# Two more blocks of each norm's modulation as dot products, and head and softmax scaling moved to ScalarE, in a hybrid DiT step

## The chip, the cores and the metric

One Trainium2 chip, one core. The metric is the device time of one launch in microseconds (us), the median of several runs. The engines are TensorE (PE, with its weight loads as PEld), VectorE (DVE), ScalarE (ACT), GpSimd (POOL) and SyncE (SP, which here only issues DMAs).

## The reference

One layer of a diffusion backbone, on 128 context tokens (stream s=0) and 128 latent tokens (s=1), width 2048, in fp32. The six modulation vectors of a stream come from its condition; RMSNorm is scaled and shifted with them before each sub-layer:

```python
sh1, sc1, g1, sh2, sc2, g2 = ada_mod(c, w_ada, b_ada)      # silu(c) @ w_ada + b_ada, split in 6
h = rms_norm(x, norm1_w) * (1 + sc1) + sh1
qa, ka, va, qb, kb, vb, ga, gb = project_heads(h, w_in, ...) # q and k are RMS-normed per head of 128
...                                                          # softmax attention, mixers A and B
x = x + g1 * merge_branches(oa, ob, ga, gb, w_br_a, w_br_b, w_out)
h2 = rms_norm(x, norm2_w) * (1 + sc2) + sh2
x = x + g2 * (relu(h2 @ w_up) ** 2 @ w_down)
```

Mixer A is windowed attention with two key heads and a sink logit in the softmax, mixer B a neighbourhood attention with eight heads and a position bias; latent queries also see a cache of 128 context keys.

## The kernel before, in words

**Steps.** All large products run over a list of *steps*, 456 in all: one weight tile of 128 x 1024 fp32 (512 KB), 12 matmuls of 512 columns each. For precision each weight is used as a high part and a low part: ACT copies the tile into wH (`copy`, line 101), DVE subtracts to wL (line 260), and three matmuls (wH·hH, wL·hH, wH·hL) replace one. For steps in the table `LO_DMA` the low part is made without DVE: ACT writes the negative of wH (line 266) and a POOL DMA loads the weight once more and adds it (line 267).

**Order of the steps.** `begin` does steps 0 to 2; then the input projection runs in chunks of its 16 k-tiles (`CHUNKS`, 2, 2, 2, 4, 6), so that it can start before all of the modulated input h exists: steps 0 to 8 need k-tiles 0 and 1, 9 to 17 the next two, then 18 to 26, 27 to 44 and 45 to 71. The gates are steps 72 to 135, the branch products 136 to 167, the output product 168 to 199, the rest the two layers of the MLP.

**Modulation.** Shift and scale of a block of 128 columns (an *fb*) come in one of two ways. *As matmuls*: `mod_pair` loads eight tiles of w_ada ("araw") for two blocks (`pair_load`, line 322), multiplies them with the padded conditions (`pair_mm_q`, line 330: the profile counts 64 per pair), copies the result to SBUF (`ada_evac`), transposes it back into columns (`ada_cols`, line 348, into "ps_sel") and finishes with three small DVE operations (lines 351 to 358). `make_h` then modulates xnT (ACT line 378, DVE line 376) and `split_h` makes hL (line 105). The first `FB1` blocks of norm 1 go this way, pair f at step `ADA_AT[f]` (pair 0 in `begin`), and the first `FB_DVE` blocks of norm 2, half a pair at each step of `SS_AT`. *As dot products*: `dot_load` (line 1398) loads transposed rows of w_ada ("aT"), `load_cond` (line 1392) spreads half a condition over the partitions ("cB", two tiles), and DVE reduces the product to one column per stream (`dot`, line 1411). The rest of the blocks go this way, and so do the gates g1 and g2. A dot job takes two dots at neighbouring steps; each block needs two jobs for shift and two for scale.

**Attention.** `qk_stat` squares q or k (ACT, line 671), reduces per head (DVE, line 673) and takes the inverse root; `qk_apply` scales the heads of stream 0 on ACT (line 683) and those of stream 1 on DVE (line 684). There are seven such units, 26 heads per stream. An attention job has the stages scores (PE, line 756), softmax (ACT exponentials with accumulated sums, line 781), `normalise` (DVE scales four rows of probabilities at once, line 795), transposed probabilities (PE line 802, copied by ACT into "probT") and values (PE, line 809 for mixer A, 813 for B); eight jobs, four rows of 128 or 256 each.

**What sets the order.** Each engine executes in program order. At step i, `run` first issues the loads of all steps up to i + RUN[i] on SP's queue, then prepares high and low parts up to i + LOOK[i], then issues the matmuls, then whatever the tables put at that step: `DOTS1` (dots of norm 1), `DOTS` (of g1 and norm 2), `DOTS2` (of g2), `ADA_AT`, `SS_AT`, `POST` (stat, apply and transpose of each unit), `JOBS` (the five stages of the eight jobs). SP's queue is in that order too, and a few transfers are in flight at once.

Of the kernel before, what the change touches and what calls it, by code (L numbers as in the profile page):

```python
# [47 lines left out]
GATE2_USE = 3  # L48
ROW_AT = [5, 5, 9, 5]
DIRECT = (3,)  # L50
LO_DMA = [88, 106, 116, 131, 165, 180, 184, 196, 218, 224, 230, 232, 250, 251, 256, 282, 283, 288, 314, 315, 320, 329, 346, 347, 352, 378, 379, 384, 392, 410, 416, 442, 443, 449, 450]
LO_AHEAD = 2

LOOK = "652322414122454322223333333122333442223323122555465644344534355765215632223444456685566655544323333333321122122312343545666445443333342344444444444434556566643344457766322234414766567565566546555331235663226676666666656665554444444444444444555555555555555544433333333344445555555555555555444444444444444455555555555555554444433244444444555555555555555546444444444444445555555555555555444444444445555555666465555555554444446656654585434443744464222433444444"
RUN = "411111111111121323334444433333333312222233465566655466545667777556664445555776765655445445555656776654432333333312444444555566553333333343334455555566655655555655666575565577788866677666665653476544343366555566666666666666665555555555554444566666666666666655555555555555556666666666666666555555555555555566666666555666665555577555555555666666666666666655555555555555556666666666666666555577755555575454566666676555566666666665555555776766555535444666666666"
CONST_AT = [65, 69]
ADA_AT = [None, 5, 13, 16, 21, 37, 32]
XS_AT = {1: 13, 2: 19, 3: 31}
POST = {('kvA', 0): [67, 71, 76], ('qA', 0): [70, 73, 78], ('qA', 1): [72, 74, 83], ('kB', 0): [76, 86, 90], ('qB', 0): [82, 84, 93], ('kB', 1): [87, 90, 98], ('qB', 1): [90, 93, 96]}
JOBS = [[80, 81, 81, 88, 94], [79, 83, 88, 90, 92], [87, 87, 89, 95, 100], [93, 93, 96, 102, 105], [96, 97, 100, 105, 112], [102, 103, 107, 112, 123], [105, 107, 111, 118, 123], [112, 115, 118, 121, 123]]  # L60
SS_AT = [44, 57, 75, 75, 139, 139]
T_AT = [3, 4]
PREP_IN = [5, 7]
DOTS = [32, 44, 47, 47, 49, 50, 51, 52, 53, 56, 58, 60, 67, 67, 68, 69, 77, 78, 84, 85, 92, 93, 93, 94, 95, 99, 100, 103, 103, 104, 108, 110, 111, 111, 116, 118, 120, 120, 121, 122, 126, 126, 128, 129, 130, 132, 134, 137, 137, 138, 138, 143, 144, 145, 151, 155, 155, 158, 160, 160, 166, 167, 173, 173, 174, 175, 176, 178, 179, 180, 183, 190]
DOTS2 = [234, 237, 240, 266, 269, 272, 298, 301, 329, 330, 332, 363, 364, 367, 397, 398, 424, 426, 426, 428, 429, 431, 431, 432, 432, 436, 439, 439, 440, 441, 444, 444]
STAT_AT = [-1, 0, 8, 11]
T_PAIR = [[6, 8], [6, 8], [8, 10], [5, 7], [10, 13], [8, 14], [12, 9]]
# [10 lines left out]
def tile_hybrid_step(ctx: ExitStack, tc: tile.TileContext, a):  # L78
# [98 lines left out]
    r = SM(2, "r")  # L177
# [104 lines left out]

    by_dma = sorted(LO_DMA)

    def run():
        loads.sort(key=lambda x: x[:2])
        for st in wsteps:
            while loads and loads[0][0] <= st["i"] + int(RUN[st["i"]]):
                loads.pop(0)[2]()
            for j in sorted(j for j in pre if j <= st["i"]):  # L290
                for fn in pre.pop(j):
                    fn()
            to = st["i"] + int(LOOK[st["i"]]) + 1
            while by_dma and by_dma[0] < to + LO_AHEAD:
# [372 lines left out]
    def qk_stat(u, nh):  # L667
        raw = units[u]
        sq = G("sq").rearrange("p (s h d) -> p s h d", s=2, d=HD)[:, :, 0:nh, :]
        for s in range(2):  # L670
            act.activation(sq[:, s].rearrange("p h d -> p (h d)"), raw[:, s, 0:nh * HD], AF.Square)
        ssq, r = SM(2 * nh, "ssq"), SM(2 * nh, "rq")
        dve.tensor_reduce(ssq.rearrange("p (s h) -> p s h", s=2), sq, axis=AX.X, op=OP.add)
        rsqrt(r, ssq, HD * EPS)
        qk[u] = sq, r

    def qk_apply(u, nh):

        name, raw = u[0], units[u]
        x4 = raw.rearrange("p s (h d) -> p s h d", d=HD)[:, :, 0:nh, :]  # L680
        sq, r = qk.pop(u)
        for h in range(nh):
            act.activation(x4[:, 0, h, :], x4[:, 0, h, :], AF.Copy, scale=r[:, h:h + 1])
        dve.tensor_tensor(x4[:, 1], x4[:, 1], r[:, nh:2 * nh].unsqueeze(2).to_broadcast([P, nh, HD]), op=OP.mult)
# [47 lines left out]
    def att_job(mix, s, g):  # L732
        st = {}
        nb = 1 + s
        nk = P * nb
# [53 lines left out]
        def normalise():  # L789
            den, prob = st["den"], st["P"]  # L790
            if mix == "A":
                dve.tensor_tensor(den, den, st["es"], op=OP.add)
            rd = SM(4, "rd")
            dve.reciprocal(rd, den)
            dve.tensor_tensor(prob[:, :, 0:nk], prob[:, :, 0:nk], rd.unsqueeze(2).to_broadcast([P, 4, nk]), op=OP.mult)
# [706 lines left out]
    ex(placed[-1][0] + 2, dot_end)  # L1502
# [104 lines left out]
```

## Time and profile before

| | |
|---|---|
| median of 3 runs | 1323.73 us (1323.15 to 1325.13) |
| profiled execution | 1324.28 us |
| its span | 1322.5 us |
| busy in the span: PE, DVE, ACT, POOL | 1309.0, 1151.4, 890.8, 87.1 us |
| DMA traffic | 419.03 MB, 317 GB/s on the mean, 408 GB/s between 33 and 132 us |
| matmul records of the modulation pairs (line 330) | 640, 38.5 us busy |

The span is what the profiler sees between the first and the last instruction; the execution's time is 1.78 us longer. A busy time is the sum of an engine's instructions with overlaps removed. In the groups, "idle before" is how long the engine had stood still when the group's instructions began, and the arrow names what ended it. In the timelines consecutive instructions of one kind are one row, with their count behind an x. "SPq" and "POOLq" are the queues on which DMAs are issued.

### The profile page before, as it was taken

What the parts mean: (1) busy time and instruction counts of PE and PEld (TensorE: products, weight loads), DVE (VectorE), ACT (ScalarE), POOL (GpSimd) and SP (SyncE); (2) the same over time, 40 slices, a digit from 0 to 9 for tenths busy, and PEclk for the clock granted to TensorE, in tenths of its full rate; (3) what the DMA queues carried; (4) which work ended last, traced back from release to release, by engine and by line L of the source; (5) the groups of instructions that cost most, each with busy time, mean ns of one, the idle gap of its engine ahead of it and who ended that gap; (6) DMA issues with size and microseconds to landing.
All of it is one profiled execution on the core that took longest, in us unless ns stands there. A gap on an engine that the chain in (4) does not pass through costs nothing.

```text
span 1322.5 us, 18220 instructions
## 1 busy us (share of the span) xinstructions
PE 1309.0 (99%) x6388; PEld 1061.3 (80%) x6388; DVE 1151.4 (87%) x1487; ACT 890.8 (67%) x1129; POOL 87.1 (7%) x109
## 2 busy tenths in 40 slices
PE   8999999999999999999999999999999999999998
PEld 4777788788888878888888888888888888888876
DVE  4578699988898999999789889898898998979996
ACT  5634656576565545755788877968879688796772
POOL 0000000512000000000100010100101001010011
PEclk9999999999999999999999999999999999999999
DMA  9999998887689999998489998888998799899996
GB/s 375 408 408 409 406 398 344 326 286 281 200 296 343 373 377 349 323 374 306 137 289 291 290 312 273 283 300 289 292 321 281 282 341 288 295 269 366 375 334 185
DMA packets 155260, 419.03 MB, mean 317 GB/s; under 512 B 52720, under 2 KB 53984, under 8 KB 155168
## 3 DMA queue, kind: packets, MB, share of 16 engines
q1 hardware_dynamic: 146128, 386.54, 80.1%
q0 software_dynamic: 8848, 31.23, 10.3%
q8 instruction: 50, 0.82, 0.2%
q14 instruction: 42, 0.34, 0.1%
q10 hardware_dynamic: 192, 0.10, 0.0%
HBM read 390.24 MB, written 17.61 MB: 308 GB/s over the span
## 4 chain that ended last, share of the span: by engine, by line
PE 93%; DMA 3%; DVE 2%; issue 1%; POOL 0%; ACT 0%; POOLq 0%; DVEq 0%; ACTq 0%
PE acc L313 16%; PE acc L314 16%; PE acc L315 16%; PE Q L1191 6%; PE Q L1192 6%; PE Q L1193 6%; PE acc L424 5%; PE acc L425 5%; PE acc L426 5%; PE ps_ada L330 2%; DMA araw<-in_w_pair 2%; PE ps_S L756 1%; DMA wL<-in_w_down 1%; DVE aT L1411 1%; PE acc L1026 1%
## 5 line engine op out<-in xcount | busy, mean ns | idle before, releaser
L101 ACT ACTIVATE wH<-raw 128x1024 fp32r<-128x1024 f32 (+1 forms) x376 | 381.0, 1045 | 126.4 <-DMA raw<-in_w_in 17.0
L260 DVE TENSOR_TENSOR wL<-raw,wH 128x1024 fp32r<-128x1024 f32 x335 | 399.1, 1223 | 47.8 <-ACT wH L101 32.7
L424 PE MATMUL acc<-wH,hH 128*128 128x512 f32 x276 | 109.1, 395 | 0.0
L426 PE MATMUL acc<-wH,hL 128*128 128x512 f32 x276 | 107.6, 390 | 0.0
L425 PE MATMUL acc<-wL,hH 128*128 128x512 f32 x276 | 107.5, 390 | 0.0
L313 PE MATMUL acc<-wH,hH 128*128 128x512 f32 x256 | 102.6, 401 | 0.0
L315 PE MATMUL acc<-wH,hL 128*128 128x512 f32 x256 | 99.8, 390 | 0.0
L314 PE MATMUL acc<-wL,hH 128*128 128x512 f32 x256 | 99.7, 390 | 0.0
L1411 DVE CUSTOM_DVE_ANT_0 junk<-aT,cB,cols 128x1024 bf16<-128x1024 f32 x56 | 71.3, 1283 | 1.4 <-DMA cB<-silu 1.4
L1411 DVE CUSTOM_DVE_ANT_0 aT<-aT,cB,cols 128x1024 f32<-128x1024 f32 x56 | 71.6, 1288 | 0.2
L424 PEld LDWEIGHTS acc<-wH,hH 128*128 128x128 f32 x276 | 51.8, 188 | 13.6 <-issue 3.3
L1256 DVE TENSOR_TENSOR tL<-t,tH 128x1024 fp32r<-128x1024 f32 x42 | 51.2, 1220 | 11.2 <-ACT tH L101 11.2
L426 PEld LDWEIGHTS acc<-wH,hL 128*128 128x128 f32 x276 | 51.8, 188 | 11.2 <-DVE hL L105 0.2
L101 ACT ACTIVATE uH<-raw 128x1024 fp32r<-128x1024 f32 x42 | 44.4, 1058 | 23.6 <-DVE raw L1250 21.5
L425 PEld LDWEIGHTS acc<-wL,hH 128*128 128x128 f32 x276 | 51.9, 188 | 10.3
L101 ACT ACTIVATE tH<-t 128x1024 fp32r<-128x1024 f32 x42 | 44.3, 1054 | 23.5 <-DVE t L1246 18.5
L313 PEld LDWEIGHTS acc<-wH,hH 128*128 128x128 f32 x256 | 48.1, 188 | 10.5 <-issue 1.1
L314 PEld LDWEIGHTS acc<-wL,hH 128*128 128x128 f32 x256 | 48.1, 188 | 10.0 <-issue 0.7
L315 PEld LDWEIGHTS acc<-wH,hL 128*128 128x128 f32 x256 | 48.1, 188 | 10.1
L1246 DVE TENSOR_TENSOR t<-raw 128x1024 f32<-128x1024 f32 x42 | 51.2, 1218 | 1.0 <-PE acc L314 1.0
L1238 DVE TENSOR_TENSOR XL<-raw,XH 128x1024 fp32r<-128x1024 f32 x42 | 51.2, 1218 | 0.6 <-DMA sm<-dsum 0.5
L1256 DVE TENSOR_TENSOR uL<-raw,uH 128x1024 fp32r<-128x1024 f32 x42 | 51.1, 1218 | 0.0
(630 smaller groups left out, 3374.4 us busy)
## 6 DMA issues: line engine op xcount, KB each, us to landing
raw<-in_w_in SPq DMA_DIRECT2D x133, 512.0 KB, 9.0
raw<-in_w_down SPq DMA_DIRECT2D x128, 512.0 KB, 6.6
raw<-in_w_upF SPq DMA_DIRECT2D x84, 512.0 KB, 6.3
araw<-in_w_pair SPq DMA_DIRECT2D x80, 512.0 KB, 10.1
aT<-in_w_gT SPq DMA_DIRECT2D x64, 512.0 KB, 8.9
aT<-in_w_adaT SPq DMA_DIRECT2D x48, 512.0 KB, 9.9
raw<-in_w_up SPq DMA_DIRECT2D x44, 512.0 KB, 6.2
raw<-in_w_out SPq DMA_DIRECT2D x32, 512.0 KB, 10.2
```

The costliest lines, as they stand in the source:

```text
L101: act.activation(out, in_, AF.Copy)
L260: dve.tensor_tensor(st["lo"], st["raw"], st["hi"].bitcast(F32), op=OP.subtract)
L313: pe.matmul(acc[tb], sh, wh[:, k, :], start=f, stop=False, **kw)
L314: pe.matmul(acc[tb], sh, wl[:, k, :], start=False, stop=False, **kw)
L315: pe.matmul(acc[tb], sl, wh[:, k, :], start=False, stop=l, **kw)
L424: pe.matmul(acc[tb], sh, wh[:, k, :], start=kt == 0 and k == 0 and not held and not seeded, stop=False, **kw)
L425: pe.matmul(acc[tb], sh, wl[:, k, :], start=False, stop=False, **kw)
L426: pe.matmul(acc[tb], sl, wh[:, k, :], start=False, stop=last and k == 1 and not hold, **kw)
L1191: pe.matmul(acc, stat[0], hi, start=f, stop=False)
L1192: pe.matmul(acc, stat[0], lo, start=False, stop=False)
L1256: dve.tensor_tensor(b[n + "L"], v, b[n + "H"].bitcast(F32), op=OP.subtract)
L1411: dve.tensor_tensor_reduce(out, box["raw"], cB[s, tag], 1.0, dst if second else baT[:, part, fb:fb + 1], OP.mult, OP.add, dst)
```

## The change

- `FB1` 14 to 12 and `FB_DVE` 6 to 4: two blocks of norm 1 (one pair) and two of norm 2 (two half pairs) become dot products. 16 araw loads and 64 matmuls less in the program (128 of the profile's records, which count each twice), 16 more aT loads, 32 more dots.
- `qk_stat`: a square per head with an accumulated sum on ACT (52) in place of 14 squares and seven DVE reductions. `qk_apply`: ACT scales the heads of both streams, DVE no longer does. `normalise`: four ACT copies with a scale per job in place of one DVE operation.
- Tables anew. Pair 1 stands at step 3, no longer at 5; the dots of norm 1 are 16 jobs from step 8 on, formerly 8 from step 26 on; five more steps have their low part by DMA; `LOOK` and `RUN` differ in many places.

```diff
-FB_DVE = 6
-FB1 = 14
+FB_DVE = 4
+FB1 = 12
-DOTS1 = [26, 26, 29, 36, 39, 40, 41, 42]
+DOTS1 = [8, 8, 9, 12, 16, 18, 23, 26, 27, 28, 31, 31, 33, 35, 37, 39]
-LO_DMA = [88, 106, 116, 131, 165, 180, 184, 196, 218, 224, 230, 232, ..., 384, 392, 410, 416, 442, 443, 449, 450]
+LO_DMA = [46, 57, 74, 92, 106, 114, 116, 127, 165, 176, 184, 196, ..., 385, 410, 411, 416, 440, 442, 449]
-ADA_AT = [None, 5, 13, 16, 21, 37, 32]
+ADA_AT = [None, 3, 13, 16, 21, 35]
-SS_AT = [44, 57, 75, 75, 139, 139]
+SS_AT = [75, 75, 139, 139]
...
+        ssq, r = SM(2 * nh, "ssq"), SM(2 * nh, "rq")
         for s in range(2):
-            act.activation(sq[:, s].rearrange("p h d -> p (h d)"), raw[:, s, 0:nh * HD], AF.Square)
-        ssq, r = SM(2 * nh, "ssq"), SM(2 * nh, "rq")
-        dve.tensor_reduce(ssq.rearrange("p (s h) -> p s h", s=2), sq, axis=AX.X, op=OP.add)
+            for h in range(nh):
+                act.activation(sq[:, s, h, :], raw[:, s, h * HD:(h + 1) * HD], AF.Square,
+                               accum_out=ssq[:, s * nh + h:s * nh + h + 1])
...
-        for h in range(nh):
-            act.activation(x4[:, 0, h, :], x4[:, 0, h, :], AF.Copy, scale=r[:, h:h + 1])
-        dve.tensor_tensor(x4[:, 1], x4[:, 1], r[:, nh:2 * nh].unsqueeze(2).to_broadcast([P, nh, HD]), op=OP.mult)
+        for s in range(2):
+            for h in range(nh):
+                act.activation(x4[:, s, h, :], x4[:, s, h, :], AF.Copy, scale=r[:, s * nh + h:s * nh + h + 1])
...
-            dve.tensor_tensor(prob[:, :, 0:nk], prob[:, :, 0:nk], rd.unsqueeze(2).to_broadcast([P, 4, nk]), op=OP.mult)
+            for h in range(4):
+                act.activation(prob[:, h, 0:nk], prob[:, h, 0:nk], AF.Copy, scale=rd[:, h:h + 1])
```

Lines of the changed kernel stand two further down behind the tables' place for `dot` and its helpers (1394, 1400, 1413), one or two further in attention. Two places where the order moves:

SP's queue near the start of the program, before: the loads (issuing line, destination<-source, shape, how many) behind the first pair's, with pair 1 (the first araw row), pair 2 and pair 3.

```order
L230 DMA raw<-in_w_in 128x1024 x6
L322 DMA araw<-in_w_pair 128x1024 x8
L230 DMA raw<-in_w_in 128x1024 x8
L322 DMA araw<-in_w_pair 128x1024 x8
L230 DMA raw<-in_w_in 128x1024 x3
L322 DMA araw<-in_w_pair 128x1024 x8
```

The same place in the changed kernel, from pair 1 to pair 2:

```order
L230 DMA raw<-in_w_in 128x1024 x4
L322 DMA araw<-in_w_pair 128x1024 x8
L230 DMA raw<-in_w_in 128x1024
L1394 DMA cB_384<-silu 128x1024
L1394 DMA cB_386<-silu 128x1024
L230 DMA raw<-in_w_in 128x1024 x3
L1400 DMA aT<-in_w_adaT 128x1024 x2
L230 DMA raw<-in_w_in 128x1024
L1400 DMA aT<-in_w_adaT 128x1024
L230 DMA raw<-in_w_in 128x1024 x3
L1400 DMA aT<-in_w_adaT 128x1024
L230 DMA raw<-in_w_in 128x1024 x2
```

And from there, pair 2 to pair 3:

```order
L322 DMA araw<-in_w_pair 128x1024 x8
L230 DMA raw<-in_w_in 128x1024 x2
L1400 DMA aT<-in_w_adaT 128x1024
L230 DMA raw<-in_w_in 128x1024
L322 DMA araw<-in_w_pair 128x1024 x8
```

Pair 1 stands two step tiles further ahead; two condition broadcasts and four aT tiles have come in ahead of pair 2, one more aT tile ahead of pair 3.

ACT's queue in attention, before, from the squares of one unit of k to the copies of the second job's probabilities (the last row):

```order
L671 ACTIVATE sq<-u_kB_2335 128x512 x2
L781 ACTIVATE prob,den<-ps_S,nm 128x128 x4
L787 ACTIVATE es<-es 128x4
L101 ACTIVATE probT<-ps_PT 128x512
L101 ACTIVATE wH<-raw 128x1024 x2
L101 ACTIVATE T_kB_3124<-ps_qT 128x512
L715 ACTIVATE T_kB_3124<-ps_qT,cols 128x512
L683 ACTIVATE u_kB_2335<-u_kB_2335,rq 128x128 x4
L671 ACTIVATE sq<-u_qB_2179 128x512 x2
L101 ACTIVATE probT<-ps_PT 128x512 x2
```

The same stretch of the changed kernel:

```order
L673 ACTIVATE sq,ssq<-u_kB_2263 128x128 x8
L782 ACTIVATE prob,den<-ps_S,nm 128x128 x4
L788 ACTIVATE es<-es 128x4
L101 ACTIVATE probT<-ps_PT 128x512
L797 ACTIVATE prob<-prob,rd 128x256 x4
L797 ACTIVATE prob<-prob,rd 128x128 x4
L101 ACTIVATE wH<-raw 128x1024 x2
L101 ACTIVATE T_kB_3116<-ps_qT 128x512
L716 ACTIVATE T_kB_3116<-ps_qT,cols 128x512
L673 ACTIVATE sq,ssq<-u_qB_2102 128x128 x8
L101 ACTIVATE probT<-ps_PT 128x512 x2
```

Two rows of eight squares stand where two of two stood, and the softmax scalings of two jobs (L797) have come in between; the scaling of the k unit's heads (L683) has moved behind the copies.

More of the change, by code (lines that the diff above doesn't have):

```diff
@@ L50 @@
 DIRECT = (3,)
-LO_DMA = [88, 106, 116, 131, 165, 180, 184, 196, 218, 224, 230, 232, 250, 251, 256, 282, 283, 288, 314, 315, 320, 329, 346, 347, 352, 378, 379, 384, 392, 410, 416, 442, 443, 449, 450]
+LO_DMA = [46, 57, 74, 92, 106, 114, 116, 127, 165, 176, 184, 196, 218, 224, 228, 232, 237, 250, 251, 256, 282, 283, 288, 314, 315, 320, 329, 346, 347, 352, 378, 379, 384, 385, 410, 411, 416, 440, 442, 449]
 LO_AHEAD = 2
-LOOK = "652322414122454322223333333122333442223323122555465644344534355765215632223444456685566655544323333333321122122312343545666445443333342344444444444434556566643344457766322234414766567565566546555331235663226676666666656665554444444444444444555555555555555544433333333344445555555555555555444444444444444455555555555555554444433244444444555555555555555546444444444444445555555555555555444444444445555555666465555555554444446656654585434443744464222433444444"
@@ L55 @@
[L55 removed]
+LOOK = "652322403022443232223333212232333432223344255866576742122334355654104521223444356685566655544323344444432222122312343544555334333333342344444433444434556566643344457544102234414766567565676546555331235663226676666666656665543233333344444444555555555566666655533333333344445555555555555555444444444444443454444455555555554444433244444444555555555555555546444444444444447555555555555555444444444445555555666465555555554444346656654565434444754464233555555555"
@@ L56 @@
+RUN = "411111111111121323334466733333333312222344576677656467645667777556553434435865876875445445555656876654432333333312444444555566575533333343334455555566655655555655666575565577788866677666665653476544343366555566666666665555565555555555554466566666666666666655555555555555556666666666666666555555555555555566666666777777776555577555555555666666666666666655555555555555556666666666666666555555556666655474566666676555566666666665755555776777555534444666666666"
 CONST_AT = [65, 69]
-ADA_AT = [None, 5, 13, 16, 21, 37, 32]
+ADA_AT = [None, 3, 13, 16, 21, 35]
@@ L58 @@
 XS_AT = {1: 13, 2: 19, 3: 31}
-POST = {('kvA', 0): [67, 71, 76], ('qA', 0): [70, 73, 78], ('qA', 1): [72, 74, 83], ('kB', 0): [76, 86, 90], ('qB', 0): [82, 84, 93], ('kB', 1): [87, 90, 98], ('qB', 1): [90, 93, 96]}
-JOBS = [[80, 81, 81, 88, 94], [79, 83, 88, 90, 92], [87, 87, 89, 95, 100], [93, 93, 96, 102, 105], [96, 97, 100, 105, 112], [102, 103, 107, 112, 123], [105, 107, 111, 118, 123], [112, 115, 118, 121, 123]]
-SS_AT = [44, 57, 75, 75, 139, 139]
+POST = {('kvA', 0): [67, 71, 76], ('qA', 0): [70, 73, 78], ('qA', 1): [72, 74, 83], ('kB', 0): [76, 86, 90], ('qB', 0): [80, 84, 93], ('kB', 1): [87, 91, 99], ('qB', 1): [90, 93, 96]}
@@ L62 @@
+JOBS = [[80, 81, 81, 88, 94], [79, 83, 88, 90, 92], [87, 87, 88, 95, 100], [92, 93, 96, 102, 105], [96, 97, 100, 105, 112], [102, 103, 107, 112, 123], [105, 107, 111, 118, 123], [112, 115, 118, 121, 123]]
+SS_AT = [75, 75, 139, 139]
 T_AT = [3, 4]
 PREP_IN = [5, 7]
-DOTS = [32, 44, 47, 47, 49, 50, 51, 52, 53, 56, 58, 60, 67, 67, 68, 69, 77, 78, 84, 85, 92, 93, 93, 94, 95, 99, 100, 103, 103, 104, 108, 110, 111, 111, 116, 118, 120, 120, 121, 122, 126, 126, 128, 129, 130, 132, 134, 137, 137, 138, 138, 143, 144, 145, 151, 155, 155, 158, 160, 160, 166, 167, 173, 173, 174, 175, 176, 178, 179, 180, 183, 190]
@@ L65 @@
-DOTS2 = [234, 237, 240, 266, 269, 272, 298, 301, 329, 330, 332, 363, 364, 367, 397, 398, 424, 426, 426, 428, 429, 431, 431, 432, 432, 436, 439, 439, 440, 441, 444, 444]
+DOTS = [41, 44, 47, 47, 48, 48, 50, 51, 56, 56, 57, 58, 60, 62, 67, 67, 69, 69, 70, 73, 77, 79, 84, 84, 86, 92, 93, 93, 94, 95, 98, 99, 100, 103, 103, 106, 108, 111, 111, 112, 114, 116, 116, 118, 120, 120, 121, 122, 126, 126, 128, 129, 130, 132, 134, 137, 137, 138, 138, 143, 144, 144, 151, 155, 155, 158, 160, 160, 166, 167, 173, 173, 174, 175, 176, 178, 179, 183, 188, 190]
@@ L66 @@
+DOTS2 = [234, 237, 240, 266, 269, 272, 297, 301, 329, 330, 332, 363, 364, 367, 397, 398, 424, 426, 426, 428, 431, 431, 432, 432, 433, 436, 439, 439, 440, 441, 444, 444]
 STAT_AT = [-1, 0, 8, 11]
-T_PAIR = [[6, 8], [6, 8], [8, 10], [5, 7], [10, 13], [8, 14], [12, 9]]
-P_PAIR = [[1, 3], [2, 4], [3, 4], [-1, 3], [3, 4], [3, 6], [6, 4]]
+T_PAIR = [[10, 8], [6, 8], [8, 10], [5, 7], [10, 13], [8, 14], [12, 9]]
+P_PAIR = [[1, 3], [2, 4], [3, 4], [-1, 3], [3, 4], [3, 6], [6, 5]]
 M_TE = (3,)
@@ L72 @@
 P_UP = [2, 3]
-T_UP = [6, 11]
+T_UP = [7, 12]
 COL = {"qA": 0, "kvA": 1024, "qB": 1536, "kB": 2560, "vB": 3584, "gA": 4608, "gB": 6656}
```

## Prediction

> **What bounds the kernel now.** I read the page first: the busy line and the chain.
>
> ```profile
> span 1322.5 us, 18220 instructions
> PE 1309.0 (99%) x6388; PEld 1061.3 (80%) x6388; DVE 1151.4 (87%) x1487; ACT 890.8 (67%) x1129; POOL 87.1 (7%) x109
> PE 93%; DMA 3%; DVE 2%; issue 1%; POOL 0%; ACT 0%; POOLq 0%; DVEq 0%; ACTq 0%
> ```
>
> TensorE (PE) is the bound: 99% busy, 93% of the chain, some 13.5 us of the span without a matmul. So a matmul that goes is worth its own time, unless PE then waits for something that used to be just in time. Windows (start and end, length, then busy time of PE, PEld, DVE, ACT and POOL, clock, DMA share, GB/s) show where that is likely.
>
> ```profile
> 0.00:33.00 33.00, 28.84 (x178) 14.23 (x179) 15.76 (x34) 17.29 (x32) 3.11 (x12) 1.00 0.96 375
> 33.00:66.00 33.00, 32.37 (x193) 24.50 (x195) 16.89 (x23) 20.11 (x29) 0.00 (x0) 1.00 1.03 408
> ...
> 165.00:198.00 33.00, 33.00 (x170) 26.48 (x169) 32.86 (x46) 18.65 (x25) 0.00 (x0) 1.00 1.01 398
> ```
>
> ```profile
> 264.00:429.00 165.00, 165.00 (x848) 138.09 (x841) 143.85 (x208) 104.04 (x199) 15.21 (x13) 1.00 0.80 281
> 66.00:165.00 99.00, 99.00 (x684) 75.90 (x677) 74.64 (x116) 50.08 (x72) 0.00 (x0) 1.00 1.03 408
> ```
>
> To 198 us the DMA engines are as full as PE (share 1.01 to 1.03). VectorE (DVE) has 24 us free in 66 to 165, none in 165 to 198. In the attention stretch, 264 to 429, ScalarE (ACT) is idle for 61 us of 165, and PE for none. The longest waits of PE itself are few (total, times, longest):
>
> ```profile
> PE acc L314 <- DMA wL<-in_w_down: 1.7, 1, 1.7
> PE ps_ada L330 <- DMA araw<-in_w_pair: 1.3, 2, 0.7
> ```
>
> **The change, part by part.** *Matmuls removed.* The chain of waits has the modulation matmuls as pieces (start, us, what); PE's timeline has the selections, which make columns of them.
>
> ```profile
> 32.38 10.16 DMA araw<-in_w_pair
> 65.85 3.59 PE ps_ada L330 x64
> 171.70 1.86 PE ps_ada L330 x32
> 209.15 1.86 PE ps_ada L330 x32
> ```
>
> ```profile
> 30.27 0.39 PE L424 MATMUL acc<-wH,hH 128*128 128x512 f32 x1
> ...
> 38.53 3.42 PE L330 MATMUL ps_ada<-araw,early 128*32 128x256 f32 x56
> 42.58 0.64 PE L330 MATMUL ps_ada<-araw,early 128*32 128x256 f32 x8 [0.63 <-DMA araw<-in_w_pair]
> 43.15 0.50 PE L424 MATMUL acc<-wH,hH 128*128 128x512 f32 x1
> ...
> 46.03 0.60 PE L348 MATMUL ps_sel<-ident,S 128*128 128x128 f32 x4
> 46.38 0.48 PE L424 MATMUL acc<-wH,hH 128*128 128x512 f32 x1
> ...
> 78.25 3.66 PE L330 MATMUL ps_ada<-araw,early 128*32 128x256 f32 x64
> ```
>
> One pair of norm 1 goes (3.59), two half pairs of norm 2 (1.86 each, at steps 44 and 57) and two selections of four (46.03 to 46.38, 0.35 each, and about 0.1 of slower first matmuls behind it): 3.59 + 3.72 + 0.9 = **−8.2 us**, all on PE.
>
> *Loads of the first pairs.* Here I take more than half of it back. While the DMA engines are full, a tile lands when its place in SP's queue says. Pair 1's last tile is the chain's piece at 32.38: issued then, landed at 42.5, and PE's last eight matmuls start at 42.58, having waited for it. At 408 GB/s a 512 KB tile takes 1.285 us. The change puts those loads behind four step tiles instead of six, so the last lands 2 × 1.285 earlier, at 40.0, and its matmuls end at 40.6. But it puts the matmuls behind step 3 instead of step 5. Step 3 starts at 30.27 and is 12 matmuls 0.227 apart, 2.73 us, so PE is ready for pair 1 at 33.0 and stands waiting for tiles. Steps 4 and 5 (5.5 us), which used to cover this, come after it: step 6 starts at 46.1 instead of 43.15. **+2.9 us.**
>
> Pair 3 is next; SP's timeline (start, us, what) has the loads of pairs 2 and 3:
>
> ```profile
> 43.89 9.29 SPq L322 DMA_DIRECT2D araw<-in_w_pair  x8
> 54.12 2.87 SPq L230 DMA_DIRECT2D raw<-in_w_in  x3
> 57.94 9.24 SPq L322 DMA_DIRECT2D araw<-in_w_pair  x8
> ```
>
> Its last tile is issued at 67.1 and lands near 77.2, one microsecond before PE takes the pair at 78.25. In SP's new order, 36 tiles stand from pair 1's last to pair 3's last, where 27 did: two broadcasts of the condition (cB) and five aT tiles for the early dot products have come in. So it lands at 40.0 + 36 × 1.285 = 86.2 and its matmuls end at 86.8; PE, ready at 78.25 + 2.9, would have ended at 84.8. **+1.9 us.** Pair 2 stays covered: its last tile lands at 40.0 + 24 × 1.285 = 70.8, and PE, at it from 68.8, needs it only at 72. The pair after these is shifted no further by the queue than PE is. What is lost so early stays lost, for PE has no idle time to make it up in. Sum **+4.8**; bounds 0 (the queue moves faster than I count) and +8 (DVE late as well, next).
>
> *DVE.* By line and shape (busy us, mean ns, idle before):
>
> ```profile
> L260 DVE TENSOR_TENSOR wL<-raw,wH 128x1024 fp32r<-128x1024 f32 x335 | 399.1, 1223 | 47.8 <-ACT wH L101 32.7 <-PE acc L314 8.0 <-PE acc L315 3.7
> L1411 DVE CUSTOM_DVE_ANT_0 aT<-aT,cB,cols 128x1024 f32<-128x1024 f32 x56 | 71.6, 1288 | 0.2
> L673 DVE TENSOR_REDUCE ssq<-sq 128x8 f32<-128x1024 f32 (+1 forms) x7 | 8.0, 1139 | 2.2 <-ACT sq L671 2.2
> L684 DVE TENSOR_TENSOR u_kB<-u_kB,rq 128x512 f32<-128x512 f32 x2 | 1.4, 686 | 0.0
> L795 DVE TENSOR_TENSOR prob<-prob,rd 128x1024 f32<-128x1024 f32 x4 | 4.9, 1224 | 0.1
> L795 DVE TENSOR_TENSOR prob<-prob,rd 128x512 f32<-128x512 f32 x4 | 2.8, 692 | 0.1
> ```
>
> Thirty-two dot products come in (41 us). The seven reductions (8.0), seven scalings of 0.69 or less (4.5), the eight softmax scalings (4.9 and 2.8) and five subtractions (6.1) go out: net +15 us of a whole run in which DVE is idle 171. Sixteen of the 32 fall before 165 us: 16 × 1.22 = 19.5 of the 24 us free there, so DVE has some 5 us left. The first six stand ahead of the low-part subtractions of steps 12 and 13: their aT lands at 50.3, six take 7.5 us, and the low part of step 12 is then ready near 59, against its matmuls at 62.9. I cost this at **0**, covered by those four microseconds and, a little later, by PE's own wait for pair 3; without that cover it is +3. In 165 to 264 three more dot jobs (7.3 us) meet less other work there: three subtractions turned into DMAs, three reductions and scalings gone. Even.
>
> *ACT.* Everything taken off DVE lands here, in the attention stretch. ACT's timeline:
>
> ```profile
> 307.47 0.37 ACT L781 ACTIVATE prob<-ps_S,nm 128x128 f32<-128x128 f32 x1 [2.65 <-PE ps_PT L802]
> 307.74 0.19 ACT L781 ACTIVATION_READ_ACCUMULATOR prob<-ps_S,nm 128x1 f32 x1
> 307.83 0.36 ACT L781 ACTIVATE prob<-ps_S,nm 128x128 f32<-128x128 f32 x1
> ...
> 313.06 1.06 ACT L101 ACTIVATE wH<-raw 128x1024 fp32r<-128x1024 f32 x1 [2.55 <-PE ps_qT L709]
> ...
> 315.08 1.27 ACT L683 ACTIVATE u_kB<-u_kB,rq 128x128 f32<-128x128 f32 x4
> 316.40 1.15 ACT L671 ACTIVATE sq<-u_qB 128x512 f32<-128x512 f32 x2
> 317.46 1.06 ACT L101 ACTIVATE probT<-ps_PT 128x512 f32<-128x512 f32 x2
> ```
>
> A piece with an accumulator read takes 0.36 us in the queue (307.47 to 307.83), a scaled piece of 128 columns 0.30 (four in 1.27). A scaled piece of 256 columns has no row; between 0.30 and twice that I take 0.40. So 52 squares cost 18.7 instead of 8, 26 more head scalings 7.8, and 32 softmax pieces 16 × 0.30 + 16 × 0.40 = 11.2: +30 us, against 61 idle. The total fits; single moments may not. At the copies of the second job's probabilities (317.46), the queue from the exponentials at 307.47 on is now: exponentials and first copy 2.0, eight softmax pieces 2.8, two weight copies 2.0, T_kB 1.1, eight squares 2.8, copies. With the earlier additions (squares 1.7 and head scalings 2.5 more, less a weight copy and 2.65 of waiting) the exponentials start 0.6 later. The copies begin at 308.1 + 10.7 = 318.8, 1.3 later, and no wait is left in the queue. PE takes them here:
>
> ```profile
> 319.31 1.72 PE ps_o L809 x4
> ```
>
> The first copy ends 0.9 ahead of that now, so 1.3 late is +0.4. Behind the copies on ACT stand weight copies, with several steps of lead. Bounds for the whole stretch 0 and +8 (a microsecond for each of eight jobs); I take **+0.5**.
>
> [...]
>
> *DMA and the end.* Sixteen araw tiles are exchanged for 16 aT tiles, bytes equal. There are five more low-part reloads of 512 KB by POOL's queue, which take this long to land (last column, us):
>
> ```profile
> wL<-in_w_in POOLq DMA_DIRECT2D x4, 512.0 KB, 8.0
> ```
>
> The tightest is that of step 46, issued near 161.5 with the DMA engines full, so by 172 (as long as the 10.16 of the araw piece), against its matmuls near 174.7: nothing, with 3 us of cover. Near the end PE waits for a low part that comes by DMA (the 1.7 above); the list of such steps now ends 440, 442, 449 instead of 442, 443, 449, 450, which may remove that wait or move it: **0**, bounds −3 and +3.
>
> Sum: −8.2 + 4.8 + 0.5 = −2.9. The profiled execution took 1324.28 us (span 1322.5 and 1.78 around it): 1321.4. It lies 0.55 above the median of 1323.73, so I predict **1320.8**.
>
> **The rivals.** *One: the loads are hidden.* The full −8.2 comes, and a little more at the end (−2): 1315.5, or 1313.5. For it: in the page 128 of PE's records go and no bytes are added. Against: the row at 42.58 shows PE already waiting for pair 1, and the new order leaves PE two steps less in front of it.
>
> *Two, the slower side: ACT becomes the bound in attention.* Its place is 284 to 429 us, its price what each job's squares and scalings add in front of the copies PE waits for. It decides from the point at which more than about 1 us per job is past the slack: at 1.1 over eight jobs it is +8.8, so 1324.28 − 3.4 + 8.8 − 0.55 = 1329.1; at half of that 1324.7. For it: both long waits of ACT in that queue (2.65, 2.55) are used up by the additions. Against: 31 us idle remain over the stretch, and the new tables bring one job's scores and another's scaling a step forward.
>
> *Three: DVE is late in 50 to 165 us.* The dots ahead of low parts cost PE another 3 to 5: 1324 to 1326. For it: 5 us left of 24. Against: pair 3's wait covers the tightest place.
>
> *Four: the pieces cancel exactly*, since loads, waits and squares take all 8.2: 1323.7. It needs +3 from two or three; I count it as the upper part of the forecast.
>
> **How the numbers follow.** Chances: forecast with its small spread (1318.5 to 1323.5) 0.44; rival one 0.22; rival two 0.2; rival three 0.14. About 0.2% (2.6 us) is what a measurement of this kernel can tell from no change, so faster means below 1321.1, slower above 1326.4. Faster: 0.25 of the forecast's 0.44 and all of rival one, 0.47. Same: the forecast's other 0.19, 0.03 of rival two and 0.04 of rival three, 0.26. Slower: the rest of two and three, 0.27. The range reaches from rival one with the end's gain, 1313.5, to rival two at its full price, 1329.
>
> **What would show it.** Right: PE's waits for araw grow from 1.3 to about 6 us, in 33 to 41 and 81 to 86; step 6 starts near 46 and the norm-2 pairs' absence brings PE ahead of before from 170 us on; no PE wait in 264 to 429 above 1 us. Wrong: araw waits under 2 us (rival one), waits for T, probT or S together above 4 us (rival two), waits for wL between 50 and 165 (rival three), or a new wait of over 2 us at 1260 to 1300.

## The result, and the profile after

The changed kernel takes 1329.62 us (median of 7 runs, 1326.7 to 1331.2), the kernel before 1324.09 us on the same chip (7 runs, 1323.15 to 1325.65). The ratio is 1.004, with an interval of [1.0028, 1.0051]: slower by 0.4%. Forecast was 1320.8, the range ended at 1329.0.

First the page of the changed kernel, the same lines as before.

```profile
span 1327.7 us, 18165 instructions
PE 1305.8 (98%) x6251; PEld 1058.5 (80%) x6252; DVE 1163.4 (88%) x1515; ACT 918.7 (69%) x1279; POOL 92.8 (7%) x114
PE 87%; DMA 7%; DVE 4%; POOL 1%; issue 1%; ACT 0%; SPq 0%; ACTq 0%; POOLq 0%; DVEq 0%
```

PE is busy 3.2 us less, not 8, and the span is 5.2 us longer: the idle time of PE grew from 13.5 to 21.9 us, and some of its matmuls must have become slower. In the chain DMA has gone from 3% to 7%. PE's two longest waits (total, times, longest):

```profile
PE acc L314 <- DMA wL<-in_w_in: 5.4, 1, 5.4
PE ps_ada L330 <- DMA araw<-in_w_pair: 4.2, 7, 0.6
```

The windows (length, busy PE, PEld, DVE, ACT, POOL, clock, DMA share, GB/s) say where:

```profile
33.00:66.00 33.00, 30.12 (x172) 21.85 (x171) 17.55 (x27) 18.69 (x27) 0.00 (x0) 0.95 1.03 408
66.00:99.00 33.00, 32.36 (x241) 23.75 (x240) 28.08 (x48) 11.92 (x16) 0.00 (x0) 1.00 1.03 408
99.00:132.00 33.00, 33.00 (x196) 25.94 (x196) 32.93 (x50) 13.40 (x16) 0.00 (x0) 1.00 1.03 408
...
231.00:264.00 33.00, 27.61 (x112) 22.32 (x111) 27.63 (x39) 20.12 (x66) 23.23 (x19) 0.90 0.89 327
```

Two windows stand out, and in both the column of the clock, 1.00 everywhere in the kernel before, has fallen too: 0.95 in 33 to 66 and 0.90 in 231 to 264. To turn this into a ledger I take the start of each step's first matmul from PE's timeline in both kernels and subtract. PE of the changed kernel, behind (+) or ahead (−) of the kernel before, in us:

| step | starts before | changed | no74 | bef_act | bef_74 | no74_late | late_few | hyb | hyb2 | no74_dve |
|---|---|---|---|---|---|---|---|---|---|---|
| 7 | 46.4 | +4.8 | +3.4 | −0.4 | 0.0 | 0.0 | −0.4 | 0.0 | −0.1 | +3.2 |
| 17 | 81.8 | +5.5 | +5.0 | −0.3 | −0.1 | −0.2 | −0.6 | −0.1 | −0.1 | +4.7 |
| 28 | 116.7 | +5.5 | +5.0 | −0.3 | −0.1 | +10.5 | +10.7 | −0.1 | −0.1 | +4.7 |
| 40 | 157.9 | +1.2 | +0.7 | −0.3 | −0.1 | +6.9 | +7.1 | −0.1 | −0.1 | +0.4 |
| 60 | 217.0 | −3.5 | −4.0 | −0.3 | −0.1 | +2.3 | +2.4 | +0.2 | −3.2 | −4.3 |
| 76 | 264.2 | **+4.5** | −3.0 | 0.0 | **+7.1** | +3.2 | +3.4 | +1.8 | −3.2 | +0.9 |
| 113 | 392.2 | +5.7 | −1.8 | +5.0 | +7.1 | +4.4 | +4.6 | +3.1 | **+9.8** | +1.3 |
| 451 | 1303.8 | +4.3 | −2.8 | +3.7 | +5.2 | +2.8 | +3.9 | +2.8 | +9.6 | +0.2 |

(The columns behind "changed" are experiments, below; three more are told in the text.) To step 60 the changed kernel does what was forecast: 5 us lost early, 9 gained, 3.5 ahead. Between steps 70 and 76 it loses 8.0 us in one place and never gets them back.

That place, in PE's timeline (start, us):

```profile
251.60 0.39 PE L313 MATMUL acc<-wH,hH 128*128 128x512 f32 x1
257.38 0.79 PE L314 MATMUL acc<-wL,hH 128*128 128x512 f32 x1 [5.39 <-DMA wL<-in_w_in]
257.97 0.63 PE L315 MATMUL acc<-wH,hL 128*128 128x512 f32 x1
258.39 0.63 PE L313 MATMUL acc<-wH,hH 128*128 128x512 f32 x1
```

PE waits 5.39 us for the low part of step 74, one of the twelve steps that are new in `LO_DMA` (seven old ones are gone, which leaves five more). And behind the wait, matmuls last 0.63 us, not 0.39, and start 0.42 apart, not 0.227. Who delivers so late is in POOL's timeline:

```profile
233.18 0.58 POOL L652 TENSOR_SCALAR_AFFINE_SELECT bias<-bias 64x384 f32<-64x384 f32 x1 [44.66 <-DMA bias<-in_rpb_qk]
...
244.23 1.07 POOL L147 TENSOR_SCALAR rs<-ssq 128x4 f32<-128x4 f32 x1
245.38 1.94 POOL L148 TENSOR_TENSOR rq<-rs,pw 128x4 f32<-128x4 f32 x1
247.29 0.93 POOL L267 DMA_DIRECT2D wL<-in_w_in  x1
```

ACT had written the negative copy from 235.98 to 237.0. The DMA that completes it stands in POOL's queue behind eight masking operations on the bias, which begin when the bias has landed at 233.1, and one inverse root; it is issued at 247.29 and takes 10.0 us. The low part is there at 257.3. PE wanted it at 251.8.

### The profile page after: what moved, and what is told of

Its sections match the earlier page's. It is cut to its first block, busy times and chain, and to the rows that moved or that the text cites. A ratio compares the mean times of both kernels' runs of the same rounds, so it can differ in the third digit from the quotient of the medians.

```text
span 1327.7 us, 18165 instructions
## 1 busy us (share of the span) xinstructions
PE 1305.8 (98%) x6251; PEld 1058.5 (80%) x6252; DVE 1163.4 (88%) x1515; ACT 918.7 (69%) x1279; POOL 92.8 (7%) x114
## 4 chain that ended last, share of the span: by engine, by line
PE 87%; DMA 7%; DVE 4%; POOL 1%; issue 1%; ACT 0%; SPq 0%; ACTq 0%; POOLq 0%; DVEq 0%
PE acc L314 16%; PE acc L313 16%; PE acc L315 16%; PE Q L1194 6%; PE Q L1195 6%; PE Q L1193 6%; PE acc L424 4%; PE acc L425 4%; PE acc L426 4%; DMA araw<-in_w_pair 3%; PE ps_ada L330 2%; DMA raw<-in_w_down 1%; DVE junk L1413 1%; DVE aT L1413 1%; DVE wL L260 1%
## 5 line engine op out<-in xcount | busy, mean ns | idle before, releaser
L260 DVE TENSOR_TENSOR wL<-raw,wH 128x1024 fp32r<-128x1024 f32 x330 | 393.3, 1223 | 45.3 <-ACT wH L101 30.8
L1413 DVE CUSTOM_DVE_ANT_0 aT<-aT,cB,cols 128x1024 f32<-128x1024 f32 x64 | 81.5, 1287 | 0.1
L1413 DVE CUSTOM_DVE_ANT_0 junk<-aT,cB,cols 128x1024 bf16<-128x1024 f32 x64 | 81.5, 1288 | 0.0
L425 PEld LDWEIGHTS acc<-wL,hH 128*128 128x128 f32 x276 | 52.1, 189 | 10.5
L313 PEld LDWEIGHTS acc<-wH,hH 128*128 128x128 f32 x256 | 48.7, 190 | 10.4 <-issue 0.5
```

What stands on the lines that cost most here:

```text
L260: dve.tensor_tensor(st["lo"], st["raw"], st["hi"].bitcast(F32), op=OP.subtract)
L313: pe.matmul(acc[tb], sh, wh[:, k, :], start=f, stop=False, **kw)
L425: pe.matmul(acc[tb], sh, wl[:, k, :], start=False, stop=False, **kw)
L1413: dve.tensor_tensor_reduce(out, box["raw"], cB[s, tag], 1.0, dst if second else baT[:, part, fb:fb + 1], OP.mult, OP.add, dst)
```

## Experiments

The first four are edits of the changed kernel or of the kernel before with nothing else moved. From the fifth on, what starts from the changed kernel also has step 74 out of `LO_DMA`, as no74 has, and the last two mix tables of both kernels. Each is timed against the kernel before on its own chip. The diffs show the main lines.

**1. no74.** `LO_DMA` without 74.

```diff
-LO_DMA = [46, 57, 74, 92,
+LO_DMA = [46, 57, 92,
```

> The changed kernel, step 74 taken out of LO_DMA (DVE makes its low part again). Theory: step 74's low part waits in POOL's queue behind the bias masking, and PE then restarts at half clock; the 5.4 us wait and about 2.4 us of slow matmuls go, so 1329.6 - 7.8 = 1321.8 us, ratio to before 0.998. Rival: DVE and the DMA engines are full around 250 us and deliver the low part late in any way; then less than 3 us goes, 1326.6 us or more, with a PE wait for wL from DVE near 250 us.

Measured: 1322.21 us against 1323.37, ratio 0.9989 [0.998, 0.9999]. Against its own kernel before, the changed kernel stood at +5.5, this one at −1.2: 6.7 us for one entry of a table. At step 76 PE is 7.5 us earlier, of which 0.5 was there at step 60. The theory holds, and DVE has room for the subtraction: PE's longest wait for a low part from DVE is 0.6 us.

**2. bias78.** Step 74 stays in the list; the bias is loaded and masked later.

```diff
-CONST_AT = [65, 69]
+CONST_AT = [65, 78]
```

> The changed kernel with the bias load (and its masking on POOL) moved from step 69 to step 78; step 74's low part stays a DMA. Theory: POOL's order is the cause; the DMA for step 74 is then issued near 237 us, right behind the negative copy on ACT, lands 10 us later, before PE needs it at 251.8, and the wait goes: about 1322 us. Rival: the transfer itself is late, since the DMA engines are full there: the wait stays above 3 us, 1327 us or more. A second rival: the bias comes too late for mixer B and costs a wait of its own near 330 to 400 us.

Measured: 1322.42 us, ratio 0.9993 [0.9984, 1.0002]. POOL's row for the DMA:

```profile
236.37 0.93 POOL L267 DMA_DIRECT2D wL<-in_w_in  x1 [1.70 <-DMA raw<-in_w_in]
```

It goes out 10.9 us earlier, and no wait for a low part by DMA is left. The DMA engines are less full at that moment (share 0.11, 0.68 and 0.99 in the three windows of 3 us from 234 to 243, against 1.01 to 1.05 in 246 to 258 of the changed kernel), and the transfer lands in 6.3 us instead of 10.0. So of the 14.6 us by which the low part comes earlier, POOL's order is 10.9 and the transfer 3.7. The order alone would have done: issued at 236.37 and with 10.0 us to land, the low part is there at 246.4, and PE wants it at 251.8. Neither rival appeared.

**3. bef_74.** The entry alone, in the kernel before.

```diff
-LO_DMA = [88, 106,
+LO_DMA = [74, 88, 106,
```

> The kernel before with step 74 added to LO_DMA and nothing else. Theory: POOL's masking and one root stand in front of the DMA until 248.9 us; it lands near 259, PE needs it at 255 to 256, waits 3 to 5 us and runs at a lower clock for some 4 us behind that: 1323.4 + 6 = 1329.4 us. So the one entry costs in the kernel before about what it costs in the changed one. Rival: in the kernel before POOL is done in time, or the wait is hidden: 1323.4 us.

Measured: 1329.13 us against 1323.53, ratio 1.004 [1.0026, 1.0053]: as large a slowdown as the whole change's, from one number. POOL's row and PE's wait:

```profile
248.98 0.96 POOL L267 DMA_DIRECT2D wL<-in_w_in  x1
```

```profile
PE acc L314 <- DMA wL<-in_w_in: 4.1, 1, 4.1
```

The 248.98 could have been read off the kernel before, where POOL's timeline has the same root end at 248.96:

```profile
247.09 1.87 POOL L148 TENSOR_TENSOR rq<-rs,pw 128x4 f32<-128x4 f32 x1
```

**4. warm.** PE is kept busy while it waits for pair 1's tiles, by repeating each tile's matmuls into a scratch bank.

```diff
...
+        if "keep" in box and (j, q) != (1, 3):
...
+            for n in range(8):
+                pe.matmul(box["w"][32 * (n % 4):32 * (n % 4) + 32, 0:256], cpad[:, 4 * q + n % 4, :], raw[:, n % 4, :],
+                          start=True, stop=True, tile_position=(0, 32 * (n % 4)))
```

> The changed kernel with pair 1's matmuls repeated into a scratch bank while PE waits for the next tile (adds 56 small matmuls, leaves the result alone). Theory: PE's clock falls because PE is mostly idle from 34 to 41 us; kept busy, it stays at 1.0 and steps 4 and 5 take 2.73 us each, not 4.4; step 7 starts 1.5 to 2 us earlier. But pair 3's last tile sets PE's time at 87 us in any case, so only 0 to 0.7 us is left of it at the end: 1329 us. Rival: the clock falls for another reason and stays near 0.7 in 39 to 45 us, and the extra matmuls only add time.

Measured: 1330.41 us, ratio 1.005 [1.0035, 1.0065], no gain at the end, as expected. Windows of 3 us, the changed kernel first:

```profile
36.00:39.00 3.00, 1.37 (x20) 0.41 (x24) 0.00 (x0) 0.00 (x0) 0.00 (x0) 1.00 1.02 408
39.00:42.00 3.00, 2.36 (x18) 1.02 (x19) 0.00 (x0) 0.57 (x1) 0.00 (x0) 0.72 1.01 401
42.00:45.00 3.00, 3.00 (x11) 2.35 (x11) 0.00 (x0) 2.24 (x5) 0.00 (x0) 0.71 1.03 411
```

and warm:

```profile
36.00:39.00 3.00, 3.00 (x64) 1.80 (x60) 0.00 (x0) 0.00 (x0) 0.00 (x0) 1.00 1.03 406
39.00:42.00 3.00, 3.00 (x64) 1.80 (x60) 0.00 (x0) 0.92 (x1) 0.00 (x0) 1.00 1.03 410
42.00:45.00 3.00, 3.00 (x23) 2.14 (x16) 0.00 (x0) 1.69 (x5) 0.00 (x0) 1.00 1.02 406
```

Busy through the wait, PE keeps its clock, as the theory has it. But step 7 starts 5.0 us late, no earlier than the changed kernel's 4.8, since with the additional matmuls in front of it step 4 starts 1.4 us later; that part failed. And step 17 starts 4.7 late in place of 5.5. The kept clock doesn't show the theory either: no74, with nearly the same gaps (PE busy 1.56 of 3 us in 36 to 39) and no additional matmuls, kept 1.00 as well and was 1.4 us earlier at step 7. So did bias78 (1.58) and no74_dve (1.71). At this spot the clock falls in one profile and not in another.

**5. no74_late and late_few.** Pairs 1 to 3 get back the queue they had; the first dots start at step 18.

```diff
-ADA_AT = [None, 3, 13, 16, 21, 35]
+ADA_AT = [None, 5, 13, 16, 21, 35]
-DOTS1 = [8, 8, 9, 12, 16, 18, 23, 26,
+DOTS1 = [18, 18, 19, 20, 21, 22, 24, 26,
```

> The changed kernel without step 74 in LO_DMA, with pair 1 at step 5 again and the first dot jobs of norm 1 at steps 18 to 24 in place of 8 to 23, so that pairs 1 to 3 have the loads in front of them that they had before. Theory: the early loss of 5.5 us comes from pair 1 and pair 3 arriving late in SP's queue and goes; with the 7.8 us of step 74 that makes 1329.6 - 7.8 - 5 = 1317 us, ratio 0.995. Rival: the DMA engines are full to 165 us, so that the bytes put off are missing later; then PE waits for raw or wL between 85 and 165 us and 1321 to 1323 us is left.

Measured: 1327.9 us, ratio 1.0037 [1.0023, 1.0052]. The early loss does go (step 17: −0.2), and twice as much returns at once: +5.2 at step 22 behind pair 4's loads, +10.5 at step 28. The rival was right in kind. To see whether bytes or DVE's time are missing there, late_few leaves seven of the aT loads out and lets the dots read another tile.

```diff
-                box = {}
-                load_at(i - 2, lambda box=box, job=job, h=h: dot_load(box, job, h))
+                if name == "a" and 0 < run_.index((i, (job, h, second))) < 8 and r == 0:
+                    box = first_box
+                else:
+                    first_box = box = {}
+                    load_at(i - 2, lambda box=box, job=job, h=h: dot_load(box, job, h))
```

> The kernel of no74_late (1327.9 us) with seven of its early aT loads left out: the first eight dot jobs all read the first job's tile, so these dots are computed on other rows and the modulation comes out different; DVE's work is unchanged. Theory: no74_late lost 5 us at step 22 because pair 4 stood behind six more tiles in SP's full queue; that goes, and PE is no more than 3 us behind the kernel before at step 28, where it was 10.5 behind. Rival: DVE, with 32 dots in 100 to 165 us, is what PE waits for; then 7 us or more remain at step 28.

Measured: 1329.46 us, ratio 1.0043 [1.0029, 1.0057]. The loss at step 22 halves (+2.3), but at step 28 PE is just as late, +10.7. Its window, and PE's waits between 90 and 140 us:

```profile
99.00:132.00 33.00, 26.50 (x109) 19.88 (x102) 32.86 (x52) 9.49 (x12) 0.00 (x0) 0.90 0.81 306
```

```profile
PE acc L424 <- DVE u_qA L437: 2.6, 2, 1.8
PE acc L424 <- DVE u_vB L437: 2.5, 1, 2.5
PE acc L425 <- DVE wL L260: 1.8, 2, 1.4
```

The DMA share has dropped to 0.81 (1.03 in no74_late) and DVE is full: it is DVE that PE waits for. My theory of the queue alone fell; with the dots at these later steps DVE is the next bound behind the DMA engines.

**6. pair1_load3.** Pair 1's matmuls at step 5, its loads where the change put them.

```diff
-ADA_AT = [None, 3, 13, 16, 21, 35]
+ADA_AT = [None, 5, 13, 16, 21, 35]
-            load_at(i, lambda j=j: pair_load(box, 0, k0 + j))
+            load_at(3 if f == 1 else i, lambda j=j: pair_load(box, 0, k0 + j))
```

> The changed kernel without step 74 in LO_DMA, pair 1's matmuls back at step 5, while its loads keep their place in SP's queue. Theory: while the DMA engines are full, a count of tiles in SP's queue sets PE's time, not the place of the matmuls: pair 1 costs nothing now (step 7 starts 1 us before the kernel before), but pair 3 then waits about 5 us for its last tile, which lands at 86, and from step 17 on PE is as late as without this edit, 4.3 to 5 us. So 1321.5 us, against 1322.2. Rival: the wait at pair 1 and the slow clock behind it are a loss of their own; then 4 us are gained, 1318 us.

Measured: 1325.66 us, ratio 1.0015 [1.0005, 1.0024]; neither theory. PE's wait and the chain behind it:

```profile
PE acc L424 <- ACT u_qB L101: 7.0, 1, 7.0
```

```profile
30.82 10.16 DMA raw<-in_w_in
...
41.01 1.06 ACT wH L101
42.06 0.49 ACT u_qB L101
```

A weight tile, which now stands behind the eight of pair 1, lands at 41; ACT copies it before it frees the accumulators that PE needs. PE then is 8.7 to 8.8 us late from step 6 to 28, with a granted clock of 0.50 between 39 and 48 us. So this step tile, too, was just in time, and behind the pair it makes PE wait. The run doesn't separate the two causes as meant.

**7. bef_act and no74_dve.** The three moves to ACT alone in the kernel before, and taken back in no74 (the minus lines of the change's `qk_stat`, `qk_apply` and `normalise` put in, or their plus lines).

> The kernel before with only the squares, head scalings and softmax scalings moved to ACT (its own tables). Theory: the move costs PE 1 to 3 us in attention, since ACT's queue in front of the copies of the second job's probabilities grows, and gains nothing, since DVE holds nobody up there: 1323.4 + 2 = 1325.4 us. Rival: DVE's 20 us less let low parts come earlier and the total is unchanged or better: 1323.4 us or less.

> The changed kernel without step 74 in LO_DMA, with the squares, head scalings and softmax scalings back on DVE and ACT as before (new tables). Theory: ACT's queue holds PE up by 1 to 2 us between 284 and 365 us in the changed kernel, since the chain runs through ACT from 284 to 316; with its 30 us of work back on DVE that goes: 1322.2 - 1.5 = 1320.7 us. Rival: DVE, with 20 us more and full for most of 264 to 429, becomes the one that PE waits for, 1324 us or more.

Measured: bef_act 1328.53 us against 1323.4, ratio 1.0038 [1.0023, 1.0053]; no74_dve 1325.72, ratio 1.0019 [1.0009, 1.0028]. In bef_act PE's wait and ACT's timeline:

```profile
PE ps_o L811 <- ACT probT L101: 3.1, 1, 3.1
```

```profile
311.36 1.73 ACT L797 ACTIVATE prob<-prob,rd 128x256 f32<-128x256 f32 x4
...
321.75 1.10 ACT L101 ACTIVATE probT<-ps_PT 128x512 f32<-128x512 f32 x2
```

The copies of the second job's probabilities start at 321.75 where they started at 317.46. With the old tables, then, the move costs 5.0 us at step 94, the 3.1 of waiting and slower matmuls behind it (clock 0.95 in 297 to 330). That is more than I expected, at just the spot that the prediction named. In no74_dve the rival came true, at another place:

```profile
PE acc L314 <- DVE wL L260: 3.9, 3, 3.3
```

Of these waits the 3.3 is at step 75, where DVE, with the reductions back, is late. From step 75 to 76 PE loses 5.2 us (no74: 1.0); from 76 to 113 it loses 0.4 (no74: 1.2). So with the tables of the changed kernel the moves to ACT are worth some 3 us, and with them PE is 0.8 slower in attention.

**8. hyb and hyb2.** Norm 2's half of the change alone. hyb has `FB1`, `ADA_AT`, `DOTS1` and the first 44 entries of `LOOK` and `RUN` as before and the rest as changed, without 46 and 74 in `LO_DMA`; hyb2 has the old tables to step 74, no low part by DMA before 92, and the old `DOTS` with eight more jobs, at 81, 86, 89, 96, 98, 101, 106 and 113.

```diff
-FB1 = 12
+FB1 = 14
...
-LO_DMA = [46, 57, 74, 92,
+LO_DMA = [57, 92,
...
```

> Only norm 2's half of the modulation change: FB1 14, ADA_AT and DOTS1 and the first 44 entries of LOOK and RUN as before, the rest as changed, steps 46 and 74 not in LO_DMA. Theory: the pair of norm 1 gains 4 us and costs 5 in the stage in which DMA and DVE are full, the halves of norm 2 gain 4 us free; without norm 1's part PE is level with the kernel before up to step 40 and 4 us ahead from step 60, less 1 to 2 us lost to ACT's queue: 1323.4 - 4 + 1.5 = 1321 us. Rival: three more dot jobs in 165 to 264 us are too much for DVE; then PE waits for wL there and 1323 us or more results.

> Norm 2's half of the modulation change alone, with the tables of the kernel before up to step 74 (FB1 14, ADA_AT, DOTS1, LOOK, RUN), no low part by DMA before step 92, the eight additional dot jobs spread over steps 81 to 113 where the moves to ACT leave DVE room, and the attention tables as changed. Theory: level with the kernel before to step 44, 1.9 us ahead from 45 and 3.9 ahead from 60, none of the DVE waits that the first hybrid had at steps 45 to 50; 1 to 2.5 us lost in attention to ACT's queue; 1323.4 - 3.9 + 1.5 = 1321 us, better than both kernels. Rival: with eight dot jobs in attention DVE is late there instead: waits for wL, and 1324 us or more.

Measured: hyb 1327.66 us against 1323.4, ratio 1.0034 [1.0021, 1.0047]; hyb2 1334.37 against 1323.53, ratio 1.0078 [1.0064, 1.0091]. hyb loses 4.8 us between steps 45 and 50, where PE waits for low parts (1.7) and for hL (1.2), both from DVE, which is as full in 165 to 198 as in the kernel before (32.80 of 33 us): its rival. hyb2 has the gain in full (−2.1 at step 45, −3.75 at 58), and then loses 13 between steps 76 and 113. Its longest wait there:

```profile
PE ps_S L757 <- DVE oLA L820: 4.2, 1, 4.2
```

Scores wait for a buffer that DVE is late to empty. DVE isn't full there (26.64 of 33 us in 330 to 363) and has itself waited for ACT's weight copies, so what began the delay stays open. Both rivals in their times: the matmuls of norm 2 are worth what the forecast said, but eight dot jobs fit at neither of these places with these tables. Other places weren't tried.

## Why the prediction failed

*The matmuls removed, −8.2: right.* From step 28 to 60 the changed kernel gains 9.0 us (+5.5 to −3.5). That is the pair, the two halves and their selections, and a little more.

*The early loads, +4.8: right in sum, not in its terms.* At step 17 it was +5.5. Pair 1's wait was as worked out; PE's timeline:

```profile
40.19 0.99 PE L330 MATMUL ps_ada<-araw,early 128*32 128x256 f32 x8 [0.64 <-DMA araw<-in_w_pair]
41.11 0.80 PE L424 MATMUL acc<-wH,hH 128*128 128x512 f32 x1
41.70 0.63 PE L425 MATMUL acc<-wL,hH 128*128 128x512 f32 x1
...
45.55 0.49 PE L424 MATMUL acc<-wH,hH 128*128 128x512 f32 x1
48.41 0.39 PE L424 MATMUL acc<-wH,hH 128*128 128x512 f32 x1
...
86.74 0.64 PE L330 MATMUL ps_ada<-araw,early 128*32 128x256 f32 x8 [0.64 <-DMA araw<-in_w_pair]
```

The last tile's matmuls start at 40.19, where 40.0 was forecast. But they run at the lower clock and so does most of step 4 (0.72 and 0.71 in 39 to 42 and 42 to 45): it takes 4.4 us in place of 2.73, step 6 starts at 48.4 in place of 46.1, and +4.8 had come together by step 7, where +2.9 was forecast. Pair 3's last tile then sets PE's time at 86.74 (forecast 86.2), so that only 0.7 is added there, not 1.9. Two errors cancelled, since the second wait is to a fixed time; that the sum is near is luck in this profile. In no74, where the clock stayed at 1.00, the two terms are +3.4 and +1.6, near what was worked out.

*DVE at no cost: right as the tables stand, and closer than I put it.* No wait for low parts of steps 12 and 13 shows, and in 66 to 165 DVE is left with 5 us, as worked out. But all of them lie before 99: it is busy 32.93 of 33 us in 99 to 132, and again in 132 to 165. no74_late shows what a shift of a few steps costs there.

*ACT +0.5: right at the place it named, too small for the stretch.* From step 76 to 113 the changed kernel loses 1.2 us. Only 0.3 of it falls between steps 92 and 94, at the copies that the prediction priced at +0.4. The other 0.9 falls between steps 102 and 103, and PE's only wait in the stretch stands there:

```profile
PE ps_S L757 <- DVE rd L795: 0.7, 1, 0.7
```

It is for a small DVE operation that stands behind dots, a cause that had no term in attention. That the second rival is real shows in bef_act, at 5.0. It is the tables, not ACT's idle total, that keep it small.

*The end, 0: right in sum.* The wait of 1.7 us is gone, small ones of 0.5 to 0.6 stand in the last steps, and from step 113 to the last matmul the changed kernel gains 0.4.

*The step that failed* is the sentence on the DMAs: "There are five more low-part reloads", "The tightest is that of step 46 ... nothing, with 3 us of cover". I worked out one of the new entries ahead of the end, by the load of the DMA engines, set the cost of all at 0, and did not look at the queue that issues them. For step 46 the working came out, on a POOL that had nothing else to do:

```profile
163.02 0.94 POOL L267 DMA_DIRECT2D wL<-in_w_in  x1 [150.75 <-ACT wL L266]
```

Issued at 163.0, with 9.3 us to land, it was there at 172.3 (forecast 172). Step 74's reload stands behind 14 us of work on POOL: 5.4 us of waiting and, with the restart at the lower clock (0.50 in 258 to 261), 8.0 us from step 70 to 76 (no74: 1.0). Without that entry, no74 stands 1.2 us below its own kernel before on the medians and 2.2 by the profiles' spans (1320.3 against 1322.5), where the sum was −2.9. As to the rivals: the slower side came, 5.5 above the kernel before, and not from ACT, DVE or the tail but from POOL, which none of them named.

*The clock* was in no term. In the profile before it is 1.00 in every window, so nothing there warned of it; but a forecast that has PE wait for some microseconds must reckon with it. At step 74 PE stood idle for 5.4 us; behind that, matmuls started 0.42 apart in place of 0.227 for 4.8 us (clock 0.50 in 258 to 261), 2.3 us lost:

```profile
252.00:255.00 3.00, 0.00 (x0) 0.00 (x0) 2.93 (x5) 3.00 (x14) 2.93 (x5) 1.00 1.05 274
258.00:261.00 3.00, 3.00 (x9) 2.32 (x8) 2.16 (x3) 0.00 (x0) 0.00 (x0) 0.50 1.03 418
```

Whether the clock falls behind a pause, and for how long, these runs show at single places only: bef_74 lost 2.5 us behind a wait of 4.1, and at pair 1 the clock fell in one profile and not in others with nearly the same gaps.

*The 0.40 us for a scaled piece of 256 columns* was my choice between 0.30 and twice that; the kernel before has no row of such a piece. bef_act has four in 1.73 us (311.36, above), 0.40 apart in step.

*What stays open:* why the changed kernel's runs spread over 4.5 us, where those of before spread over 2.5. The clock at pair 1 fell in one profile and not in another, and the slowest run of the changed kernel has the lowest mean clock (1331.2 us, 0.994), the fastest one of the highest (1326.7, 0.997). But no74's three runs at 0.997 (1321.4 to 1322.2 us) are no slower than its two at 1.000 (1322.2 and 1323.1), so the clock alone doesn't explain a spread. And no run here settles whether norm 1's pair can be had without its early cost.

## What to carry to other kernels

An edit that adds DMAs has to be followed on the engine that issues them: what stands ahead in that engine's queue, when it ends, plus the landing time, against the moment of need, for every one of them and not for the one that looks tightest. Where PE, DVE and the DMA engines are all full in one stretch, time freed on one of them can meet the next bound at once (from no74_late to late_few the DMA share in 99 to 132 fell from 1.03 to 0.81, and PE at step 28 was 10.7 us late in place of 10.5); count a gain only up to the first such bound, and expect each shift of a table to meet another. Price a wait of PE with the matmuls behind it: here 5.4 us of waiting cost another 2.3, in bef_74 4.1 another 2.5.

## What the runs showed of the hardware

PE's clock fell in the changed kernel without one long pause, too: from 34 to 41 us its gaps were 0.3 to 0.65 us each, PE was busy 1.37 of 3 us in 36 to 39, and the granted clock was 0.71 to 0.72 on the mean of 39 to 45, with matmuls 0.42 apart. In no74, bias78 and no74_dve almost the same gaps (busy 1.56 to 1.71 of 3) left it at 1.00. With redundant matmuls in the gaps (warm) it was 1.00 too, which one profile can't tell from chance.

The low part of step 74, a DMA of 512 KB issued by POOL, took 10.0 us to land when issued at 247.3, with the DMA engines full (share 1.01 to 1.05 in 246 to 258), 10.4 us in bef_74, and 6.3 us in bias78, issued at 236.4 with the engines less full. In the kernel before, four such DMAs took 8.0 us on the median. The place in POOL's queue cost more (10.9 us) than the slower landing (3.7).
